# One level of Strassen's algorithm in the MLP down-projection of a two-layer hybrid DiT block

## The chip, the cores and the metric

The kernel runs on one core of a Trainium2 chip. The metric is the device time of one execution in microseconds (us). TensorE (PE) does the matrix products, VectorE (DVE), ScalarE (ACT) and GpSimd (POOL) the elementwise work, and SyncE (SP) issues the DMAs.

## The reference, cut to what matters

Two layers of a hybrid block run over 512 latent and 256 context tokens of width 1024, in fp32. Attention, convolution and a state space model come first; the change does not touch them. Behind them stands an MLP with a squared ReLU and 4096 hidden units. In layer 0 it is computed for latent and context rows, in layer 1 for latent rows alone.

```python
D_MODEL, SEQ, DEPTH, CTX_LEN = 1024, 512, 2, 256
D_FF = 4 * D_MODEL

def squared_relu_mlp(t, w1, w2):
    return jnp.square(jax.nn.relu(t @ w1)) @ w2
...
    for l in range(DEPTH):
        with_ctx_out = l < DEPTH - 1
...
        f_lat = squared_relu_mlp(modulate(rms_norm(h, g_pre_mlp), sh2, sc2), w_mlp_in[l], w_mlp_out[l])
        h = h + g2 * rms_norm(f_lat, g_post_mlp)
        if with_ctx_out:
...
            f_ctx = squared_relu_mlp(modulate(rms_norm(hc, g_pre_mlp), sh2c, sc2c), w_mlp_in[l], w_mlp_out[l])
```

## The kernel before

**Arithmetic.** An fp32 value is split into a high half, which is the value rounded to the matmul's fp32r type, and a low half, which is the rest. `mm3` (L638 to L641) forms a product by three matmuls: high times high, high times low, low times high.

**Weights.** They go through one ring of ten tiles of 128 x 1024, all named `w` (`wtile`, L610). `wload` (L614) loads raw tiles by SP's queue (L620), rounds each on ACT to a high tile (L623) and subtracts to a low tile (L624), on DVE and POOL in turn. So each weight tile passes three tiles of the ring. `blocks` (L630) gives the tiles of one call the shape that the products want.

**The MLP** (`phase_mlp`, from L1364) goes through the 4096 hidden units in eight groups of four blocks of 128. For a group, `get1` loads four blocks of `w_mlp_in`, and `mlp1` (L1383) computes a block of hidden values: 24 matmuls for the 512 latent columns and, in layer 0, 24 more for the 256 context columns. They end in PSUM tiles `ps_m`; ACT takes the ReLU (L1391), DVE squares (L1392), ACT and DVE split the result (L1394, L1395). `get2` loads four blocks of `w_mlp_out`. The down-projection then goes over the token tiles of 128 rows: 4 blocks x 3 matmuls in each of two halves of 512 output columns, into a PSUM tile `ps_q` of 1024 columns. DVE adds it to an accumulator in SBUF, `facc` (L1469; a tile named `g`). Group 0 copies in place of adding. Group 7 also has the output norm and the residual (L1463 and on).

**Beside it.** In layer 0, groups 1 to 3 carry steps that prepare layer 1's state space model (`E.npr`), and groups 4 to 7 the adaptive modulation of layer 1, eight raw tiles a group through the same ring with four small matmuls each (L755, `E.ada1`).

**The order.** Nothing is placed by hand: the tile scheduler sets each engine's order from the program text and its own estimates of time. PSUM has three tiles `ps_m`, one `ps_a` and two `ps_q` in this phase. A tile of a ring is free again when its last reader is done, and a load into it waits for that.

## Time and profile before

| | |
|---|---|
| time, median of 3 runs | 1655.72 us (1654.39 to 1658.1) |
| time of the profiled execution | 1657.21 us |
| its span in the trace | 1655.4 us |
| mean granted TensorE clock | 0.969 of full speed |
| PE busy | 1559.4 us, 94%, 8872 matmuls |
| DVE busy | 900.2 us, 54% |
| ACT busy | 552.5 us, 33% |
| POOL busy | 302.5 us, 18% |
| loads of w_mlp_in, w_mlp_out | 64 of 512 KB each |

The span is what the trace covers; the time of the same execution is 1.8 us longer. Busy shares are means over all stages of the kernel, and a matmul's busy time includes its overlap with the next, so the distance between starts tells its price. All rows below are of this one execution.

### The profile page before, as it was taken

To read this page: it belongs to the slowest core of one execution; us is meant where nothing else is said; L and a number is where in the kernel's file an instruction comes from. 1 tells how busy PE (TensorE), PEld (TensorE's weight loads), DVE (VectorE), ACT (ScalarE), POOL (GpSimd) and SP (SyncE) were. 2 spreads that over 40 slices of the span, in tenths; PEclk is the share of its full clock that TensorE was granted. 3 is DMA by queue.
4 is the path that set the end of the run, shared out by engine and by line. 5 is a ranking of instruction groups with operands and counts; after the bars stand their busy time and mean duration, and the time that the engine had idled before them with its cause. 6 is when DMAs were issued, how large, how long until landed. Compare 5 with 4: busy or idle time off the path is not lost.

```text
span 1655.4 us, 22621 instructions
## 1 busy us (share of the span) xinstructions
PE 1559.4 (94%) x8872; PEld 1258.4 (76%) x8872; DVE 900.2 (54%) x1986; ACT 552.5 (33%) x1037; POOL 302.5 (18%) x231
## 2 busy tenths in 40 slices
PE   5899999899999999999999988999898999999997
PEld 2677876667888888877788866687676888888885
DVE  8776538677965553232333376753775733333335
ACT  5321235655413213030321344212564433322222
POOL 0000221022211111110111135013102322212222
PEclk9999999999999999999999998979899999999999
DMA  9466311015232222263511245831203232222223
GB/s 347 144 217 212 112 52 52 1 52 186 97 112 87 94 70 77 98 225 112 203 51 51 91 187 177 303 110 54 100 1 113 92 102 92 90 98 102 102 89 127
DMA packets 72986, 193.80 MB, mean 117 GB/s; under 512 B 15152, under 2 KB 25648, under 8 KB 72496
## 3 DMA queue, kind: packets, MB, share of 16 engines
q1 hardware_dynamic: 72880, 192.37, 33.4%
q8 instruction: 69, 1.13, 0.3%
q14 instruction: 37, 0.30, 0.1%
HBM read 172.15 MB, written 20.19 MB: 116 GB/s over the span
## 4 chain that ended last, share of the span: by engine, by line
PE 77%; DVE 13%; ACT 4%; DMA 3%; issue 2%; POOL 1%; SPq 0%; DVEq 0%; ACTq 0%; POOLq 0%
PE ps_m L639 14%; PE ps_m L641 14%; PE ps_m L640 14%; PE ps_q L640 8%; PE ps_q L639 8%; PE ps_q L641 8%; PE ps_a L755 3%; ACT p L872 2%; PE ps_s L526 2%; PE ps_t L897 2%; DVE p L864 1%; DMA w<-in_w_ada 1%; DVE p L877 1%; PE ps_t L890 1%; DMA ssm_tr<-strips 1%
## 5 line engine op out<-in xcount | busy, mean ns | idle before, releaser
L624 POOL TENSOR_TENSOR w<-w 128x1024 fp32r<-128x1024 f32 x79 | 193.1, 2444 | 785.9 <-ACT w L623 345.0
L623 ACT CAST w<-w 128x1024 fp32r<-128x1024 f32 x172 | 179.0, 1050 | 454.0 <-PE ps_q L640 293.2
L640 PE MATMUL ps_q<-w,f 128*128 128x512 f32 x640 | 249.1, 391 | 1.9 <-DVE w L624 1.1
L639 PE MATMUL ps_q<-w,f 128*128 128x512 f32 x640 | 247.4, 392 | 2.9 <-DVE g L1463 2.6
L641 PE MATMUL ps_q<-w,f 128*128 128x512 f32 x640 | 247.2, 390 | 0.0
L624 DVE TENSOR_TENSOR w<-w 128x1024 fp32r<-128x1024 f32 x93 | 115.9, 1247 | 150.2 <-ACT w L623 136.7
L639 PE MATMUL ps_m<-g,w 128*128 128x256 f32 (+1 forms) x544 | 177.3, 331 | 2.4 <-DVE g L712 2.4
L640 PE MATMUL ps_m<-g,w 128*128 128x256 f32 (+1 forms) x544 | 178.9, 330 | 0.0
L641 PE MATMUL ps_m<-g,w 128*128 128x256 f32 (+1 forms) x544 | 177.1, 329 | 0.0
L640 PE MATMUL ps_m<-f,w 128*128 128x512 f32 (+1 forms) x464 | 170.4, 368 | 0.3 <-POOL f L715 0.3
L641 PE MATMUL ps_m<-f,w 128*128 128x512 f32 (+1 forms) x464 | 170.3, 368 | 0.0
L639 PE MATMUL ps_m<-f,w 128*128 128x512 f32 (+1 forms) x464 | 170.0, 371 | 0.0
L1469 DVE TENSOR_TENSOR g<-g,ps_q 128x1024 f32<-128x1024 f32 x60 | 73.3, 1221 | 177.1 <-PE ps_q L641 177.1
L639 PEld LDWEIGHTS ps_q<-w,f 128*128 128x128 f32 x640 | 119.9, 188 | 29.1 <-DVE g L1463 3.9
L640 PEld LDWEIGHTS ps_q<-w,f 128*128 128x128 f32 x640 | 120.5, 188 | 27.5 <-DVE w L624 2.0
L641 PEld LDWEIGHTS ps_q<-w,f 128*128 128x128 f32 x640 | 120.5, 188 | 24.9
L639 PE MATMUL ps_m<-w,f 128*128 128x512 f32 (+1 forms) x336 | 124.0, 371 | 8.9 <-DVE p L917 4.0
L641 PE MATMUL ps_m<-w,f 128*128 128x512 f32 (+1 forms) x336 | 123.4, 369 | 0.0
L640 PE MATMUL ps_m<-w,f 128*128 128x512 f32 (+1 forms) x336 | 121.8, 364 | 0.0
L1392 DVE SCALAR_TENSOR_TENSOR relu<-ps_m,relu 128x512 f32<-128x512 f32 (+1 forms) x104 | 58.5, 565 | 115.9 <-ACT relu L1391 115.6
L639 PEld LDWEIGHTS ps_m<-g,w 128*128 128x128 f32 x544 | 103.1, 192 | 16.0 <-DVE g L712 3.0
L640 PEld LDWEIGHTS ps_m<-g,w 128*128 128x128 f32 x544 | 104.2, 192 | 11.5 <-issue 1.6
(285 smaller groups left out, 2557.5 us busy)
## 6 DMA issues: line engine op xcount, KB each, us to landing
w<-in_w_ada SPq DMA_DIRECT2D x88, 512.0 KB
w<-in_w_mlp_in SPq DMA_DIRECT2D x64, 512.0 KB
w<-in_w_mlp_out SPq DMA_DIRECT2D x64, 512.0 KB
w<-in_w_out SPq DMA_DIRECT2D x16, 512.0 KB
w<-in_w_conv SPq DMA_DIRECT2D x12, 512.0 KB
h_d<-g SPq DMA_DIRECT2D x12, 512.0 KB
w<-in_w_q SPq DMA_DIRECT2D x8, 512.0 KB
f<-h_d SPq DMA_DIRECT2D x8, 512.0 KB
```

The source lines that it names most:

```text
L526: nc.tensor.matmul(out(g), U[d].o[rows, q, k].rearrange("p t i -> p (t i)"), sp[d][rows, q, k, lo:NCH], start=False, stop=d == 1 and q == ...
L623: nc.scalar.copy(hi, raw)
L624: (nc.gpsimd if turn % 2 and E.wpool else nc.vector).tensor_sub(lo, raw, hi.bitcast(F32))
L639: nc.tensor.matmul(out, lh, rh, start=first, stop=False)
L640: nc.tensor.matmul(out, lh, rl, start=False, stop=False)
L641: nc.tensor.matmul(out, ll, rh, start=False, stop=last)
L755: nc.tensor.matmul(pa[32 * b:32 * b + 32, k * 256:(k + 1) * 256], E.cT[:, kc], raw[k][:, b * 256:(b + 1) * 256], start=kc == 0 and k == 0, ...
L864: V.tensor_tensor_reduce(out=p[i][:, :nk * P], in0=pq[:, l0:768], in1=E.mask[:, moff:moff + nk].rearrange("p a b -> p (a b)"), scale=0.125 ...
L872: nc.scalar.activation(p[i][:, :nk * P], p[i][:, :nk * P], AF.Exp, bias=nm[:, i:i + 1], accum_out=sm[:, i:i + 1])
L897: nc.tensor.matmul(po[e * 64:(e + 1) * 64, :256], vv, pr[:, :, e], start=j == 0, stop=j == nk - 1)
L1392: V.scalar_tensor_tensor(out=s, in0=pt, scalar=0.0, in1=s, op0=OP.max, op1=OP.mult)
L1469: V.tensor_add(facc[t], facc[t], pq)
```

## The change

In groups 1 to 6 of both layers the latent rows' down-projection is done by one level of Strassen's algorithm in Winograd's form. The 512 token rows, the 512 hidden units of the group and the 1024 output columns are each halved. Seven products of quarters, or of sums and differences of quarters, take the place of eight. A product here is `times`: 2 token tiles x 2 hidden blocks x 3 matmuls of 512 columns. Three PSUM tiles collect them (X, Y, Z, from the two buffers `ps_q`), and partly accumulated tiles are added to the accumulators on DVE, 14 sums of 512 columns a group in place of 4 of 1024.

The sums of weight quarters are taken in place in the raw tiles (`w2_forms`), the sums of hidden quarters in the fp32 hidden tiles (`h_forms`). Each of the seven forms (eight in layer 0, which needs r12 for the context) is then split by `halves_split`, the weights' low halves on DVE and POOL in turn. In layer 1 three of the weight forms have tiles of their own (`wx`, six of 128 x 1024); in layer 0 all go through the ring of ten. Context rows keep the plain product (`plain`), and their up blocks now all come ahead of the latent ones. Groups 0 and 7 stay as they were.

```diff
@@ -641,6 +641,76 @@
     nc.tensor.matmul(out, ll, rh, start=False, stop=last)
+def halves_split(E, wt, src, turn):
+    hi, lo = (wt([P, 2, 512], F32R) for _ in range(2))
+    for i, x in enumerate(src):
+        E.nc.scalar.copy(hi[:, i], x)
+        (E.nc.gpsimd if (i + turn) % 2 else E.nc.vector).tensor_sub(lo[:, i], x, hi[:, i].bitcast(F32))
+    return hi, lo
+def w2_forms(E, views, ctx):
+    nc = E.nc
+    V = nc.vector
+    raw = []
+    for v in views:
+        raw.append(wtile(E, [P, 1024]))
+        nc.sync.dma_start(raw[-1], v)
+    q = {(j, n): [raw[2 * j + i][:, n * 512:(n + 1) * 512] for i in range(2)] for j in range(2) for n in range(2)}
+    def sub(o, x, y):
+        for i in range(2):
+            V.tensor_sub(q[o][i], q[x][i], q[y][i])
+    F = {}
+    wx = E.wx if E.nwx else lambda s, d: wtile(E, s, d)
+    wt = lambda s, d: wtile(E, s, d)
+    F["r11"] = halves_split(E, wt, q[0, 0], 0)
+    F["r21"] = halves_split(E, wt, q[1, 0], 1)
+    if ctx:
+        F["r12"] = halves_split(E, wt, q[0, 1], 0)
+    F["r22"] = halves_split(E, wx, q[1, 1], 1)
+    sub((0, 0), (0, 1), (0, 0))
+    sub((0, 1), (1, 1), (0, 1))
+    sub((1, 1), (1, 1), (0, 0))
+    F["t2"] = halves_split(E, wt, q[1, 1], 0)
+    F["t1"] = halves_split(E, wx, q[0, 0], 1)
+    sub((1, 0), (1, 0), (1, 1))
+    F["t3"] = halves_split(E, wt, q[0, 1], 0)
+    F["t4"] = halves_split(E, wx, q[1, 0], 1)
+    return F
+def h_forms(E, hf):
+    nc = E.nc
+    V = nc.vector
+    q = {(i, j): hf[j][:, :, i * 256:(i + 1) * 256] for i in range(2) for j in range(2)}
+    F = {}
+    def split(name, x):
+        f = E.f4([P, 2, 2, 256], F32R)
+        nc.scalar.copy(f[:, 0], x)
+        V.tensor_sub(f[:, 1], x, f[:, 0].bitcast(F32))
+        F[name] = f
+    split("l11", q[0, 0])
+    split("l12", q[0, 1])
+    split("l22", q[1, 1])
+    V.tensor_add(q[1, 1], q[1, 0], q[1, 1])
+    V.tensor_sub(q[1, 0], q[0, 0], q[1, 0])
+    V.tensor_sub(q[0, 0], q[1, 1], q[0, 0])
+    split("s2", q[0, 0])
+    split("s1", q[1, 1])
+    split("s3", q[1, 0])
+    V.tensor_sub(q[0, 1], q[0, 1], q[0, 0])
+    split("s4", q[0, 1])
+    return F
 def sq_sum(E, x, acc, dump=None):
     if dump is None:
         dump = E.sm.tile([P, 512], BF16, name="dump", tag="dump", bufs=2)[:, :x.shape[1]]
@@ -932,6 +1002,7 @@
     E.nada, E.ada1 = 2, {4: 4, 5: 4, 6: 4, 7: 4}
     E.steps = ((0, 2, 2, 5, 8), (1, 1, 1, 3, 4))
     E.npr = {1: 3, 2: 2, 3: 2}
+    E.fast = (range(1, 7), range(1, 7))
     with ExitStack() as ctx:
         E.cst = ctx.enter_context(tc.tile_pool(name="cst", bufs=1))
         E.sm = ctx.enter_context(tc.tile_pool(name="sm", bufs=1))
@@ -1380,6 +1451,80 @@
     ada = ada_steps()
     prep = ssm_spill(E) if l == 0 else iter(())
+    E.nwx = 0 if both else 6
+    E.wx = lambda shape, dt: E.g4p.tile(shape, dt, name="wx", tag="wx", bufs=E.nwx)
+    def strassen(g):
+        hf = [E.f4([P, 2, NL]) for _ in range(2)]
+        hx = [E.f4([P, 4, NCX], F32R) for _ in range(2)] if both else None
+        def up(c, w, sg):
+            n, A = (NL, aL) if sg == 0 else (NCX, aC)
+            pt = E.pt('m')[:, :n]
+            for kc in range(8):
+                mm3(nc, pt, w[0][:, kc], w[1][:, kc], A(0, kc), A(1, kc), kc == 0, kc == 7)
+            s = E.t2([P, 512])[:, :n]
+            nc.scalar.activation(s, pt, AF.Relu)
+            o = s if sg else hf[c // 2][:, c % 2]
+            V.scalar_tensor_tensor(out=o, in0=pt, scalar=0.0, in1=s, op0=OP.max, op1=OP.mult)
+            if sg:
+                nc.scalar.copy(hx[0][:, c], s)
+                V.tensor_sub(hx[1][:, c], s, hx[0][:, c].bitcast(F32))
+        w = []
+        for k in range(2):
+            w.extend(blocks(E, w1, g * 4 + k * 2, 2, 8))
+            for _ in range(E.ada1.get(g, 0)):
+                next(ada, None)
+        for _ in range(E.npr.get(g, 0)):
+            next(prep, None)
+        for sg in ((1, 0) if both else (0,)):
+            for c in range(4):
+                up(c, w[c], sg)
+        R = w2_forms(E, [w2[g * 4 + c] for c in range(4)], both)
+        L = h_forms(E, hf)
+        def plain(hf_):
+            cs = slice(hf_ * 512, (hf_ + 1) * 512)
+            for t in (4, 5):
+                js = slice((t % 4) * P, (t % 4 + 1) * P)
+                pt = E.pt('m')
+                for c in range(4):
+                    r = R[f"r{c // 2 + 1}{hf_ + 1}"]
+                    mm3(nc, pt, hx[0][:, c, js], hx[1][:, c, js], r[0][:, c % 2], r[1][:, c % 2], c == 0, c == 3)
+                V.tensor_add(facc[t][:, cs], facc[t][:, cs], pt)
+        X, Y, Z = (E.pt('q') for _ in range(3))
+        def times(bank, l, r, first, i, n):
+            cs = slice(n * 512, (n + 1) * 512)
+            f, (rh, rl) = L[l], R[r]
+            for th in range(2):
+                o = bank[:, th * 512:(th + 1) * 512]
+                js = slice(th * P, (th + 1) * P)
+                for c in range(2):
+                    kw = dict(skip_group_check=True)
+                    nc.tensor.matmul(o, f[:, 0, c, js], rh[:, c], start=first and c == 0, stop=False, **kw)
+                    nc.tensor.matmul(o, f[:, 0, c, js], rl[:, c], start=False, stop=False, **kw)
+                    nc.tensor.matmul(o, f[:, 1, c, js], rh[:, c], start=False, stop=c == 1, **kw)
+            for th in range(2):
+                a_ = facc[2 * i + th][:, cs]
+                V.tensor_add(a_, a_, bank[:, th * 512:(th + 1) * 512])
+        if both:
+            plain(0)
+        times(X, "l11", "r11", True, 0, 0)
+        times(Y, "l12", "r21", True, 0, 0)
+        if both:
+            plain(1)
+        times(X, "s2", "t2", False, 0, 1)
+        times(Z, "s1", "t1", True, 1, 1)
+        times(X, "s3", "t3", False, 1, 1)
+        times(Z, "s4", "r22", False, 0, 1)
+        times(X, "l22", "t4", False, 1, 0)
     def mlp1(h1, c, w, sg, part=None):
         n, A = (NL, aL) if sg == 0 else (NCX, aC)
         ts = part if part else slice(0, n)
@@ -1387,7 +1532,7 @@
         pt = E.pt('m')[:, :n]
         for kc in range(8):
             mm3(nc, pt, w[0][:, kc], w[1][:, kc], A(0, kc, ts), A(1, kc, ts), kc == 0, kc == 7)
-        s = E.g4p.tile([P, 512], F32, name="relu", tag="relu", bufs=2)[:, :n]
+        s = E.t2([P, 512])[:, :n]
         nc.scalar.activation(s, pt, AF.Relu)
         V.scalar_tensor_tensor(out=s, in0=pt, scalar=0.0, in1=s, op0=OP.max, op1=OP.mult)
         hi, lo = (h1[sg][q](c)[:, ts] for q in range(2))
@@ -1404,6 +1549,9 @@
         return h1
     for g in range(8):
+        if g in E.fast[l]:
+            strassen(g)
+            continue
         h1 = h1_tiles()
         ws = []
         w = []
```

The scheduler places the rest. In the names below `w` is a tile of the weights' ring, `f4` a tile of hidden values, `g4` an accumulator or an input column tile, `ps_m` and `ps_q` are PSUM tiles.

The first place is DVE in layer 1, from the last hidden block of a group into its down-projection. Before:

```order
L1392 SCALAR_TENSOR_TENSOR relu_13328<-ps_m_13303,relu_13328 128x512
L1395 TENSOR_TENSOR f4_13206<-relu_13328,f4_13204 128x512
L1392 SCALAR_TENSOR_TENSOR relu_13358<-ps_m_13333,relu_13358 128x512
L1395 TENSOR_TENSOR f4_13206<-relu_13358,f4_13204 128x512
L1469 TENSOR_TENSOR g4_11715<-g4_11715,ps_q_13375 128x1024
L1469 TENSOR_TENSOR g4_11742<-g4_11742,ps_q_13401 128x1024
L1469 TENSOR_TENSOR g4_11769<-g4_11769,ps_q_13427 128x1024
L624 TENSOR_TENSOR w_13488<-w_13483,w_13487 128x1024
```

Now, in the last such place (ps_m_13879 is the last hidden block, ps_q_13990 is X, ps_q_13991 is Y, f4_13968 is the form l12, w_14100 the low half of the next group's first w_mlp_in tile):

```order
L1470 SCALAR_TENSOR_TENSOR f4_13770<-ps_m_13879,t2_13904 128x512
L649 TENSOR_TENSOR w_13954<-w_13907,w_13953 128x512
L1514 TENSOR_TENSOR g4_12051<-g4_12051,ps_q_13990 128x512
L1514 TENSOR_TENSOR g4_12078<-g4_12078,ps_q_13990 128x512
L697 TENSOR_TENSOR f4_13968<-f4_13770,f4_13968 128x512
L697 TENSOR_TENSOR f4_13971<-f4_13770,f4_13971 128x512
L703 TENSOR_TENSOR f4_13770<-f4_13769,f4_13770 128x2x256
L624 TENSOR_TENSOR w_14100<-w_14095,w_14099 128x1024
L704 TENSOR_TENSOR f4_13769<-f4_13769 128x2x256
L1514 TENSOR_TENSOR g4_12051<-g4_12051,ps_q_13991 128x512
```

The low half of l12, which product 2 reads, now stands behind the two sums that wait for product 1, and the next group's low half behind both.

The second place is PE in the same group: the end of product 2 (Y) and the first matmuls of the next group's up-projection. Now:

```order
L1509 MATMUL ps_q_13991<-w_13921,f4_13968 128x512
L1510 MATMUL ps_q_13991<-w_13922,f4_13968 128x512
L1511 MATMUL ps_q_13991<-w_13921,f4_13968 128x512
L639 MATMUL ps_m_14119<-g4_11443,w_14099 128x512
L640 MATMUL ps_m_14119<-g4_11447,w_14099 128x512
L641 MATMUL ps_m_14119<-g4_11443,w_14100 128x512
```

The up-projection's first block stands right behind the second product; w_14099 is the high half of the tile whose raw load, w_14095, goes into the buffer that r11's form had, read by product 1 just ahead.

The third place is PE in layer 0, group 4, at the end of the second context block and the start of the third (L825 are the ada matmuls, L755 of the kernel before). Now:

```order
L825 MATMUL ps_a_6807<-w_6817,cT_74 32x256 x4
L639 MATMUL ps_m_6942<-g4_3744,w_6799 128x256
L640 MATMUL ps_m_6942<-g4_3746,w_6799 128x256
L641 MATMUL ps_m_6942<-g4_3744,w_6800 128x256
L825 MATMUL ps_a_6807<-w_6828,cT_74 32x256 x4
L825 MATMUL ps_a_6807<-w_6829,cT_74 32x256 x4
L825 MATMUL ps_a_6807<-w_6840,cT_74 32x256 x4
L825 MATMUL ps_a_6807<-w_6841,cT_74 32x256 x4
L639 MATMUL ps_m_6972<-g4_3743,w_6856 128x256
L640 MATMUL ps_m_6972<-g4_3745,w_6856 128x256
L641 MATMUL ps_m_6972<-g4_3743,w_6857 128x256
```

And before, between a context block and the latent block behind it:

```order
L755 MATMUL ps_a_6641<-w_6651,cT_74 32x256 x4
L641 MATMUL ps_m_6776<-g4_3744,w_6630 128x256
L639 MATMUL ps_m_6776<-g4_3744,w_6629 128x256
L640 MATMUL ps_m_6776<-g4_3746,w_6629 128x256
L641 MATMUL ps_m_6776<-g4_3744,w_6630 128x256
L639 MATMUL ps_m_6776<-g4_3744,w_6629 128x256
L640 MATMUL ps_m_6776<-g4_3746,w_6629 128x256
L641 MATMUL ps_m_6776<-g4_3744,w_6630 128x256
L641 MATMUL ps_m_6806<-f4_3747,w_6634 128x512
L755 MATMUL ps_a_6641<-w_6662,cT_74 32x256 x4
```

The ada matmuls, which were spread singly among the blocks, now stand together ahead of the third block, and blocks of 512 columns no longer lie between the blocks of 256.

## Rows read from the trace of the kernel before

**Rows 1.** Page: busy time of each engine, and the chain that ended last, by engine
```profile
PE 1559.4 (94%) x8872; PEld 1258.4 (76%) x8872; DVE 900.2 (54%) x1986; ACT 552.5 (33%) x1037; POOL 302.5 (18%) x231
PE 77%; DVE 13%; ACT 4%; DMA 3%; issue 2%; POOL 1%; SPq 0%; DVEq 0%; ACTq 0%; POOLq 0%
```
**Rows 2.** Windows, MLP of layers 0, 1: us, busy PE, PEld, DVE, ACT, POOL (count), clock, DMA, GB/s
```profile
490.00:970.00 480.00, 479.67 (x2615) 394.80 (x2614) 193.24 (x326) 115.58 (x183) 72.76 (x35) 1.00 0.32 110
1318.00:1622.00 304.00, 303.25 (x1337) 250.76 (x1338) 111.90 (x113) 89.95 (x112) 68.89 (x29) 1.00 0.30 104
```
**Rows 3.** Timeline of PE, layer 1: start us, us, line, op, tiles, shape [idle before <-releaser]
```profile
1399.81 0.39 PE L640 MATMUL ps_m<-g,w 128*128 128x512 f32 x1
...
1409.78 0.39 PE L640 MATMUL ps_q<-w,f 128*128 128x512 f32 x1
```
**Rows 4.** Timeline of DVE, layer 1: the first sum of a down-projection in two groups following
```profile
1367.60 1.22 DVE L1469 TENSOR_TENSOR g<-g,ps_q 128x1024 f32<-128x1024 f32 x1 [5.03 <-PE ps_q L641]
...
1411.12 1.22 DVE L1469 TENSOR_TENSOR g<-g,ps_q 128x1024 f32<-128x1024 f32 x1 [5.03 <-PE ps_q L641]
```
**Rows 5.** Groups by form, 1350 to 1590 us: form xcount | busy us, mean ns | idle before, releaser
```profile
L1469 DVE TENSOR_TENSOR g<-g,ps_q 128x1024 f32<-128x1024 f32 x22 | 26.8, 1220 | 61.6 <-PE ps_q L641 61.6
L624 DVE TENSOR_TENSOR w<-w 128x1024 fp32r<-128x1024 f32 x21 | 25.7, 1226 | 48.5 <-ACT w L623 47.2 <-DMA w<-in_w_mlp_out 1.3
L1392 DVE SCALAR_TENSOR_TENSOR relu<-ps_m,relu 128x512 f32<-128x512 f32 x23 | 15.9, 690 | 25.2 <-ACT relu L1391 25.2
L624 POOL TENSOR_TENSOR w<-w 128x1024 fp32r<-128x1024 f32 x22 | 53.2, 2419 | 181.1 <-ACT w L623 136.4 <-PE ps_m L641 44.7
L623 ACT CAST w<-w 128x1024 fp32r<-128x1024 f32 x42 | 43.7, 1052 | 132.9 <-PE ps_q L640 70.2 <-PE ps_m L640 20.4 <-PE ps_q L641 17.8
```
**Rows 6.** Groups of the whole span, same columns: a 512-wide sum, a 512-wide GpSimd operation
```profile
L1463 DVE TENSOR_TENSOR g<-g,ps_q 128x512 f32<-128x512 f32 x20 | 13.4, 684 | 12.2 <-PE ps_q L641 12.2
L1282 POOL TENSOR_TENSOR f<-f,f 128x512 f32<-128x512 f32 x10 | 13.5, 1357 | 143.2 <-ACT dump L647 143.2
```
**Rows 7.** Timeline of SP, then of ACT, layer 1: a pair of w_mlp_in loads and its casts
```profile
1424.03 0.80 SPq L620 DMA_DIRECT2D w<-in_w_mlp_in  x2
...
1427.42 1.05 ACT L623 CAST w<-w 128x1024 fp32r<-128x1024 f32 x1 [2.43 <-DMA w<-in_w_mlp_in]
1428.64 1.05 ACT L623 CAST w<-w 128x1024 fp32r<-128x1024 f32 x1 [0.17 <-DMA w<-in_w_mlp_in]
```
**Rows 8.** Timeline of ACT and DVE, layer 1: from a group's last up product to its low half
```profile
1403.18 0.60 ACT L1391 ACTIVATE relu<-ps_m 128x512 f32<-128x512 f32 x1 [1.71 <-PE ps_m L641]
...
1405.19 0.90 DVE L1395 TENSOR_TENSOR f<-relu,f 128x512 fp32r<-128x512 f32 x1 [0.69 <-ACT f L1394]
```
**Rows 9.** Timeline of DVE and POOL, layer 0: one form alone, and beside a subtraction on GpSimd
```profile
444.49 0.68 DVE L447 TENSOR_TENSOR ssm_m<-ssm_pw,ssm_c 128x512 f32<-128x512 f32 x1
449.37 2.48 POOL L624 TENSOR_TENSOR w<-w 128x1024 fp32r<-128x1024 f32 x1 [6.58 <-ACT w L623]
449.90 2.50 DVE L447 TENSOR_TENSOR ssm_m<-ssm_pw,ssm_c 128x512 f32<-128x512 f32 x1
```
**Rows 10.** Timeline of PE, start of layer 1's MLP: 256-column matmuls, at full clock
```profile
1312.80 0.28 PE L639 MATMUL ps_m<-g,w 128*128 128x256 f32 x1
...
1315.56 0.28 PE L641 MATMUL ps_m<-g,w 128*128 128x256 f32 x1
```
**Rows 11.** The chain that ended last, one piece of layer 0: start us, us, what
```profile
1066.81 1.42 PE ps_a L755 x20
```
**Rows 12.** Windows, layer 1, and timeline of PE in it: a wait, and matmuls after it
```profile
1280.00:1290.00 10.00, 8.27 (x43) 7.01 (x44) 9.89 (x21) 4.89 (x10) 4.54 (x4) 0.61 0.50 179
1280.05 1.11 PE L700 MATMUL ps_q<-ident,g 128*128 128x128 f32 x4 [4.61 <-ACT g L673]
1286.30 0.41 PE L639 MATMUL ps_m<-g,w 128*128 128x256 f32 x1
...
1287.37 0.41 PE L641 MATMUL ps_m<-g,w 128*128 128x256 f32 x1
```

## The prediction

> **What bounds the kernel now.** I read the busy shares and the chain that ended last first. TensorE is busy for 94% of the span and carries 77% of the chain; VectorE is at 54%, ScalarE at 33%, GpSimd at 18% [rows 1]. The change lies in the MLP phases, so I then read those stretches alone. In 480 us of layer 0's MLP TensorE is busy for all but 0.33 us, in 304 us of layer 1's for all but 0.75 us, at a granted clock of 1.00, which is the 2.4 GHz level [rows 2]. There is no stall to win there: the time falls only with matmuls taken out, and every wait on PE that the change brings is lost in full. The other engines have room by their sums: in layer 1's stretch DVE is busy for 111.9 of 304 us [rows 2]. What matters is which of their results PE will find late.
>
> The prices of a matmul come from the timelines. Between the two rows of [rows 3] lie 44 steps of 512 columns: 9.97 / 44 = 0.2266 us each. Between those of [rows 10] lie 23 steps of 256 columns: 2.76 / 23 = 0.12 us. A matmul of the ada steps costs 1.42 / 20 = 0.07 us [rows 11]. A layer 1 group takes 1411.12 - 1367.60 = 43.5 us [rows 4], which is 192 matmuls (96 up, 96 down) at 0.2266.
>
> **What is removed.** Seven products of 12 matmuls (2 token halves, 2 hidden blocks, 3 of a split product) stand for 96: 84 remain. That is 12 x 0.2266 = 2.72 us per group, in 12 groups 144 matmuls and 32.6 us, all on PE, all on the path. The Trainium skill (TensorE: Matmul & The Clock Gate, Part 1) states 215.7 ns from one warm 512-column matmul to the next; by that the removal would be 31.1 us. The row says 0.2266 and I stay with it.
>
> **What is added beside PE, layer 1.** Before, DVE is busy for 111.9 / 304 x 43.5 = 16 us of a group [rows 2]: 4 sums of 1.22, 4 squares of 0.69, 4 low halves of weights of 1.23 [rows 5] and 4 of hidden blocks. After, it has 44 instructions of 512 elements (14 sums into the accumulators, 4 squares, 7 low halves of weights, 8 quarter differences, 7 low halves and 4 sums for the hidden forms). The nearest row is the 512-wide sum of 0.684 in group 7 [rows 6]; so 44 x 0.68 plus 2 low halves of w_mlp_in of 1.23 give 32.4 us. GpSimd goes from 4 x 2.42 = 9.7 us [rows 5] to 2 x 2.42 plus 7 of 1.36 (the nearest row, [rows 6]) = 14.4 us. Both sums are under 43.5, so by sums alone they are hidden. They cost where something on DVE stands in a bad place.
>
> **Waits, layer 1.** The first w_mlp_in tile of the next group goes into the buffer of r11's form, so its load waits until product 1 is nearly through; PE needs its high half 14 matmuls later and its low half 16 later, 16 x 0.2266 = 3.6 us. Before, weights are loaded well ahead. The load takes 1427.42 - 1424.03 = 3.4 us from issue to cast, the cast 1.05 [rows 7], the subtraction 1.23 [rows 5], with 0.3 for the steps between: 6.0 us. PE waits 6.0 - 3.6 = 2.4 us in each group. The second wait falls in the same place and partly under the first. The low half of l12 stands on DVE behind the two sums of product 1, and those wait for all its 12 matmuls (2.7 us). So it is ready 2.7 + 2 x 0.68 + 0.68 = 4.8 us after product 1 begins, while product 2 wants it after 14 x 0.2266 = 3.2: a wait of 1.6 us where before the chain from the last product to the low half (1403.18 to 1406.09, 2.9 us [rows 8]) ran with nothing between. In the order the subtraction of the new tile comes behind these too. What this, and the later forms of w_mlp_out, add to the 2.4 I bound by 0 and 1.35 and take 0.7. So 2.4 to 3.75, taken 3.1: per group -2.72 + 3.1 = +0.38, and **+2.3 us** for six. The first changed group of layer 1 meets a ring that is still full of group 0's splits; between nothing and one late load that nothing covers (3.4 + 1.05, about 4) I take **+2**.
>
> **Waits, layer 0.** Here the context's plain products lie between: 24 + 12 + 12 + 24 matmuls, 72 x 0.2266 = 16.3 us, cover the forms. About 26 DVE instructions must be through by then, at 0.68 some 17.7, part of them before the stretch. I take 0.7 (0.2 to 1.9) at the second product and 0.5 (0 to 1.0) at t3's low half, which stands behind sums: 1.2 per group (0.2 to 2.9). Groups 1 to 3: 3 x (-2.72 + 1.2) = **-4.6 us**.
>
> In groups 4 to 6 the eight ada tiles pass through the same ring of ten. With the context's four blocks now in a row, the third block's w_mlp_in load waits for an ada matmul, and PE reaches the block after 11 matmuls of 256 columns and 20 of ada: 11 x 0.12 + 20 x 0.07 = 2.7 us. The chain is 3.4 to 4.6 for the load (first and second of a pair [rows 7]), then 1.05 and 1.23. Its low half is needed two matmuls later, so PE waits between 3.1 and 4.2; I take 3.5, nearer to the first of a pair. Before, blocks of 512 and 256 columns alternate there and give more cover. 3 x (-2.72 + 1.2 + 3.5) = **+5.9 us**.
>
> **Sum.** -4.6 + 5.9 + 2.3 + 2 = +5.6 us. The profiled execution took 1657.2 (its span 1655.4), so 1662.8; the median of the runs shown, 1655.7, lies 1.5 lower, so against that **1661**. All low ends: -7.6 + 1.7 - 1.9 + 0 = -7.8, which is 1648. All high ends: +0.5 + 13.1 + 6.2 + 4 = +23.8, which is 1679.5. In other words the 32.6 us come off PE's work and about 38 come back as waits.
>
> **Rival A, faster: loads land in time.** The two loads of [rows 7] were in the air together, and their casts began 1.22 us apart. If a lone load lands that much sooner, in 2.2 us, each of the nine late loads (6 in layer 1, 3 in layer 0) costs 1.2 less; with DVE never late besides, the low ends fall by 10.8 to -18.6, which is 1637. With half of it, 1642. It decides from the point where a group's waits fall under 2.72 us. For it: windows of the trace show the DMA engines at 0.30 [rows 2]. Against it: part of 3.4 us is fixed, and in layer 1 something waits in the same place whatever the load does. Time 1642, chance 0.25.
>
> **Rival B, slower: the clock falls.** After a wait of 4.61 us PE ran 256-column matmuls 1.07 / 5 = 0.214 us apart, the 1.2 GHz level, and the window of 10 us was granted 0.61 [rows 12]. That lasts to 1287.37 at least, 7.3 us from the end of the wait at 1280.05; half of it, 3.7 us, is lost each time. The waits forecast in groups 4 to 6 come near that length; 3 x 3.7 = 11 more gives 1672 (all twelve groups, 1705). Against it: each of my waits is split over several places and shorter than 4.61. Chance 0.12.
>
> **Rival C, slower: DVE becomes the bound.** One form of DVE took 0.68 alone and 2.50 beside a GpSimd subtraction of 2.48 that began 0.53 earlier [rows 9]: DVE stood still meanwhile. If this holds for every DVE instruction with both inputs in SBUF, 26 x 0.68 + 2 x 1.23 = 20.1 us of these and GpSimd's 14.4 can't overlap; with the 18 that read PSUM (12.2) the group takes 46.7 us, 3.2 over today's 43.5. Six groups make +19 in place of +2.3: 1678. The Trainium skill (SBUF — State Buffer, "SBUF: two separate sides") calls the shared port pair "an exclusive lock, not a bandwidth split"; the trace agrees (2.50 against 0.68). Against it: GpSimd waits for ScalarE or PE for much of its time [rows 5], so part of its work falls where DVE is idle. Chance 0.13.
>
> **How the numbers follow.** The forecast has 0.50. A measurement of this kernel tells about 0.2% from no change, 3.3 us: "same" is 1652.4 to 1659.0. The forecast's own range of 1648 to 1679.5 is centred above it: of its 0.50 I give 0.30 to slower, 0.17 to same and 0.03 to faster. A's 0.25 goes to faster, B's and C's 0.25 to slower. Faster 0.28, same 0.17, slower 0.55. The range reaches from A's lowest, 1637, to a little past C, 1684; what lies beyond is B in many groups and A with nothing late.
>
> **What would show it.** PE should have 144 matmuls less. Right: in layer 1, between the end of product 1 and the next group's up-projection, waits on PE of 2.4 to 3.75 us per group released by the weights' cast or subtraction or by L697, and a period of 43 to 44.5 us in the first sum of a group; in layer 0's groups 4 to 6 a wait of 3 us or more at the third context block, and none so long in groups 1 to 3. C would show as DVE busy without gaps and a period near 46.7; B as a granted clock under 1.00 in the MLP's windows. The forecast is wrong if the period is under 42, or the ada groups show no wait on the weights.

## The result, and the profile after

The changed kernel takes 1705.9 us (median of 4 runs, 1703.2 to 1707.1) against 1656.9 us for the kernel before (4 runs), a ratio of 1.0293 (95% interval 1.0269 to 1.0316): 49 us slower. The prediction had said 1661, from 1637 to 1684. The profiled execution took 1707.07 us, its span is 1705.1 us, 49.7 more than before's.

The page of the changed kernel, busy times and the chain by engine:

```profile
PE 1559.6 (91%) x8728; PEld 1249.1 (73%) x8728; DVE 1124.6 (66%) x2364; ACT 622.7 (37%) x1205; POOL 384.3 (23%) x297
PE 67%; DVE 20%; ACT 5%; DMA 4%; issue 2%; POOL 1%; SPq 0%; DVEq 0%; ACTq 0%; POOLq 0%
```

The 144 matmuls are gone (8872 to 8728 [rows 1]), yet PE is busy as long as before: matmuls ran slower, at a mean granted clock of 0.952 against 0.969. The windows of both MLPs (columns as in [rows 2]) say the same. Layer 0's groups 1 to 6, then layer 1's:

```profile
496.80:968.70 471.90, 450.39 (x2439) 365.93 (x2438) 292.97 (x547) 146.79 (x259) 116.62 (x73) 0.98 0.31 107
1363.40:1668.00 304.60, 290.23 (x1228) 234.55 (x1227) 226.59 (x289) 118.50 (x187) 100.47 (x57) 0.97 0.30 102
```

Before, PE was idle there for 0.33 and 0.75 us at a clock of 1.00 [rows 2]; now for 21.5 and 14.4 us, at 0.98 and 0.97. What PE waited for in layer 1's window (us in total, times, longest):

```profile
PE ps_q L1511 <- DVE f L697: 8.8, 7, 1.8
PE ps_q L1509 <- ACT f L696: 5.3, 6, 1.5
PE ps_m L641 <- DVE w L624: 0.2, 1, 0.2
```

and in layer 0's (the longest six):

```profile
PE ps_q L1510 <- DVE w L649: 7.1, 9, 1.9
PE ps_q L1510 <- POOL w L649: 4.4, 3, 2.9
PE ps_m L639 <- ACT w L623: 4.2, 3, 2.0
PE ps_a L347 <- DVE f L337: 1.4, 1, 1.4
PE ps_q L1509 <- DVE g L1514: 1.3, 3, 0.6
PE ps_m L641 <- DVE w L624: 1.3, 2, 0.8
```

One boundary in layer 1, on PE's timeline and then on DVE's, shows how a wait arises and what follows it:

```profile
1629.06 0.50 PE L1509 MATMUL ps_q<-w,f 128*128 128x512 f32 x1 [0.72 <-ACT f L696]
1629.40 0.40 PE L1510 MATMUL ps_q<-w,f 128*128 128x512 f32 x1
1630.99 0.80 PE L1511 MATMUL ps_q<-w,f 128*128 128x512 f32 x1 [1.20 <-DVE f L697]
1631.58 0.63 PE L1509 MATMUL ps_q<-w,f 128*128 128x512 f32 x1
1632.01 0.63 PE L1510 MATMUL ps_q<-w,f 128*128 128x512 f32 x1
...
1634.48 0.39 PE L1510 MATMUL ps_q<-w,f 128*128 128x512 f32 x1
1634.71 0.39 PE L1511 MATMUL ps_q<-w,f 128*128 128x512 f32 x1
```

```profile
1628.45 0.69 DVE L649 TENSOR_TENSOR w<-w 128x512 fp32r<-128x512 f32 x1 [0.59 <-POOL w L649]
1629.06 1.28 DVE L1514 TENSOR_TENSOR g<-g,ps_q 128x512 f32<-128x512 f32 x2
1630.25 1.28 DVE L697 TENSOR_TENSOR f<-f,f 128x512 fp32r<-128x512 f32 x2
```

Product 2 waits for l12's high half, then for its low half, which stands on DVE behind the two sums of product 1. After these two waits of 0.72 and 1.20 us, matmuls start 0.43 us apart until 1634.1 (the 1.2 GHz level), then 0.23 again (the 2.4 GHz level): 1.7 us lost beside the waits.

To place the rest I matched the DVE instructions that both traces have, and took the difference of their start times at four points of before: at 400 us (ahead of layer 0's MLP), 980 (its end), 1280 (ahead of layer 1's MLP) and the end. The same was done for the experiments' profiles:

| us over before in | to 400 | layer 0 MLP | layer 1 mixer | layer 1 MLP |
|---|---|---|---|---|
| changed kernel | 2.1 | 26.7 | 7.4 | 13.6 |
| e1 no Strassen | 10.3 | 9.5 | -1.0 | 2.4 |
| e2 layer 0 | 7.9 | 27.3 | 7.1 | 3.6 |
| e3 layer 1 | -0.3 | 9.8 | 2.9 | 10.8 |
| e4 own ReLU | 5.9 | 12.1 | 3.4 | 8.6 |
| e5 fill | 2.2 | 14.1 | 1.0 | 2.4 |
| e6 short chain | 1.6 | 17.6 | 4.5 | 39.5 |
| e7 forms on DVE | 1.5 | 14.0 | -6.2 | 9.4 |
| e8 alternate | 2.3 | 8.8 | 2.9 | 8.4 |
| e9 defer | 5.1 | 14.8 | 6.1 | 34.4 |
| e10 defer, DVE | 0.5 | 13.7 | -1.0 | 34.3 |
| e11 and alternate | -1.7 | 1.1 | 4.9 | 31.5 |
| e12 layer 1 only | 4.2 | -0.1 | -0.5 | 31.8 |
| e13 sums behind | 7.6 | 13.3 | 5.5 | 1.7 |
| e14 layer 1 only | 5.3 | 0.0 | -0.8 | 2.3 |
| e15 best of | 5.9 | -4.7 | 3.0 | 3.3 |
| e16 layer 1 filled | 2.0 | 0.0 | 7.0 | 2.2 |
| e17 best, filled | -0.1 | -4.1 | 3.0 | 1.4 |
| e18 layer 0 only | -0.9 | -4.5 | 3.1 | -0.3 |

No kernel changes the work of the first column, which still varies by 12 us, nor that of the mixer, which varies by 14. Nearly all of the latter arises in one stretch, 1050 to 1130 us of before. e14 and e16 are alike up to there, yet the stretch took 79.7 us at a granted clock of 0.87 in the one and 86.3 at 0.80 in the other. In before, then e14, then e16:

```profile
1050.00:1130.00 80.00, 79.27 (x614) 64.25 (x613) 52.00 (x94) 15.74 (x28) 10.38 (x14) 0.87 0.47 162
1055.20:1134.90 79.70, 79.37 (x614) 64.36 (x613) 52.17 (x94) 16.12 (x28) 10.32 (x14) 0.87 0.47 163
1052.00:1138.30 86.30, 85.34 (x614) 70.02 (x613) 52.03 (x94) 16.09 (x28) 10.41 (x14) 0.80 0.45 151
```

Whole times therefore tell little under 0.4%. The two MLP columns tell much more, for kernels that are alike in a layer agree there within 3 us (layer 0 in e4, e5 and e9: 12.1 to 14.8), and I read the experiments by them. They come from one profile of each kernel. Beside the experiments the kernel before itself ran from 1652 to 1671 us.

### The profile page after: what moved, and what is told of

Read it like the earlier page. It is cut to its first block, busy times and chain, and to the rows that moved or that the text cites. A ratio compares the mean times of both kernels' runs of the same rounds, so it can differ in the third digit from the quotient of the medians.

```text
span 1705.1 us, 23175 instructions
## 1 busy us (share of the span) xinstructions
PE 1559.6 (91%) x8728; PEld 1249.1 (73%) x8728; DVE 1124.6 (66%) x2364; ACT 622.7 (37%) x1205; POOL 384.3 (23%) x297
## 4 chain that ended last, share of the span: by engine, by line
PE 67%; DVE 20%; ACT 5%; DMA 4%; issue 2%; POOL 1%; SPq 0%; DVEq 0%; ACTq 0%; POOLq 0%
PE ps_m L639 14%; PE ps_m L640 13%; PE ps_m L641 13%; PE ps_q L1511 3%; PE ps_q L1510 3%; PE ps_q L1509 3%; PE ps_a L825 2%; ACT p L942 2%; PE ps_s L526 2%; PE ps_q L639 2%; DVE w L666 2%; DVE w L649 2%; PE ps_q L640 2%; PE ps_q L641 2%; PE ps_t L967 1%
## 5 line engine op out<-in xcount | busy, mean ns | idle before, releaser
L624 POOL TENSOR_TENSOR w<-w 128x1024 fp32r<-128x1024 f32 x55 | 137.9, 2508 | 376.0 <-ACT w L623 234.7
L623 ACT CAST w<-w 128x1024 fp32r<-128x1024 f32 x124 | 129.6, 1049 | 180.7 <-DMA w<-in_w_mlp_in 44.1
L649 POOL TENSOR_TENSOR w<-w 128x512 fp32r<-128x512 f32 x72 | 113.7, 1585 | 284.6 <-ACT w L648 277.9
L639 PE MATMUL ps_m<-w,f 128*128 128x512 f32 (+1 forms) x432 | 160.9, 376 | 8.9 <-DVE p L987 4.0
L641 PE MATMUL ps_m<-w,f 128*128 128x512 f32 (+1 forms) x432 | 161.1, 374 | 0.0
L640 PE MATMUL ps_m<-w,f 128*128 128x512 f32 (+1 forms) x432 | 160.0, 372 | 0.0
L1514 DVE TENSOR_TENSOR g<-g,ps_q 128x512 f32<-128x512 f32 x168 | 107.7, 680 | 58.0 <-PE ps_q L1511 57.9
L648 ACT CAST w<-w 128x512 fp32r<-128x512 f32 x144 | 82.4, 618 | 156.6 <-PE ps_m L640 75.0
L624 DVE TENSOR_TENSOR w<-w 128x1024 fp32r<-128x1024 f32 x69 | 84.2, 1222 | 67.3 <-ACT w L623 61.2
L639 PEld LDWEIGHTS ps_m<-g,w 128*128 128x128 f32 x544 | 107.9, 200 | 23.4 <-ACT w L623 4.8
L1510 PE MATMUL ps_q<-w,f 128*128 128x512 f32 x264 | 108.8, 412 | 11.5 <-DVE w L649 7.1
L641 PEld LDWEIGHTS ps_m<-g,w 128*128 128x128 f32 x544 | 108.0, 199 | 13.4 <-DVE w L624 2.7
L1511 PE MATMUL ps_q<-w,f 128*128 128x512 f32 x264 | 108.5, 411 | 8.8 <-DVE f L697 8.8
L640 PEld LDWEIGHTS ps_m<-g,w 128*128 128x128 f32 x544 | 108.4, 199 | 10.4 <-issue 1.2
L1509 PE MATMUL ps_q<-w,f 128*128 128x512 f32 x264 | 107.9, 410 | 7.5 <-ACT f L696 5.3
L649 DVE TENSOR_TENSOR w<-w 128x512 fp32r<-128x512 f32 x72 | 66.7, 926 | 60.5 <-ACT w L648 51.4
```

Source lines behind the costliest of these rows:

```text
L623: nc.scalar.copy(hi, raw)
L624: (nc.gpsimd if turn % 2 and E.wpool else nc.vector).tensor_sub(lo, raw, hi.bitcast(F32))
L639: nc.tensor.matmul(out, lh, rh, start=first, stop=False)
L640: nc.tensor.matmul(out, lh, rl, start=False, stop=False)
L641: nc.tensor.matmul(out, ll, rh, start=False, stop=last)
L648: E.nc.scalar.copy(hi[:, i], x)
```

## The experiments

**Which part, which layer (e1 to e4).** Beside Strassen the change moved the ReLU tile from two tiles of its own to the four tiles `t2`, which the transposes ahead of the MLP use too. It did so in `mlp1` as well, so groups 0 and 7 did not stay wholly as they were.

```diff
-    E.fast = (range(1, 7), range(1, 7))
+    E.fast = ((), ())
```

is e1; e2 and e3 empty one of the two ranges. e4 keeps both and undoes the move:

```diff
-        s = E.t2([P, 512])[:, :n]
+        s = E.g4p.tile([P, 512], F32, name="relu", tag="relu", bufs=2 if both else 1)[:, :n]
```

> No group by Strassen in either layer; what is left of the change is the ReLU tile, which is taken from the four tiles t2 that the transposes use too. Theory 1 (the shared tiles cost time outside the changed groups: in the changed kernel the traces drift apart by about 6.5 us up to the end of group 0 of layer 0, 7.4 us in layer 1's mixer and 3.4 us at the start of layer 1's MLP): 6 to 17 us over the kernel before. Rival (that drift comes from the scheduler's answer to the new products): within 3 us of the kernel before.

> Groups 1 to 6 of layer 0 alone by Strassen. If the account of the two traces holds (groups of layer 0 +22 us, drift around them 6.5 and 7.4 us): about 33 to 39 us over the kernel before, 1690 to 1696. Rival (the loss sits in layer 1, whose groups my sum put near zero): under 1675.

> Groups 1 to 6 of layer 1 alone. By the account of the two traces the layer 1 MLP costs 10.2 us from its first copy to the end, and 3.4 us ahead of it: 1668 to 1672 if the shared ReLU tiles cost nothing in layer 0; 1674 to 1684 if they do (theory 1).

> The changed kernel with the ReLU tile in tiles of its own again (two in layer 0, one in layer 1, where there is no room for two). Theory 1: 6 to 17 us less than the changed kernel, 1689 to 1700. Rival: 1703 to 1709, no different.

Measured against 1658.8 for the kernel before: e1 1674.4 (ratio 1.0079, 1.0053 to 1.0105), e2 1696.9 (1.0199), e3 1686.7 (1.0149), e4 1685.8 (1.0147, 1.0121 to 1.0173). In the table each layer's loss comes with that layer's own change: layer 0's column is 27.3 in e2 and 9.8 in e3, layer 1's 3.6 and 10.8 (e3 came out 3 us above the higher of its two ranges). So with no Strassen product at all the kernel loses 13 us, and with Strassen but ReLU tiles of its own the loss falls from 49 us to some 25 (27 by the medians, 24 by the ratio). e1's PE timeline shows the place, at the start of layer 0's MLP, where before had no wait over 1.7 us:

```profile
434.19 1.12 PE L770 MATMUL ps_q<-ident,g 128*128 128x128 f32 x4 [4.43 <-ACT g L743]
441.69 0.58 PE L639 MATMUL ps_m<-g,w 128*128 128x256 f32 x1 [1.58 <-DVE t L1537]
```

The ReLU's square (L1537) releases the PSUM tile that the next block wants, and the transposes (L770) no longer have hidden blocks to run beside. The changed kernel has the same two waits, 4.4 and 1.6 us; in e4 both are gone. From here on every kernel has its own ReLU tiles.

**The clock (e5).** Eight dead matmuls go between products 1 and 2 of each layer 1 group:

```diff
+        if not both:
+            pa = E.pt('a')
+            for _ in range(8):
+                nc.tensor.matmul(pa, L["l11"][:, 1, 1, P:], R["r11"][0][:, 0], start=True, stop=True)
         times(Y, "l12", "r21", True, 0, 0)
```

> e4_relu_own, with 8 dead matmuls of 512 columns put on PE between products 1 and 2 of each group of layer 1 (their result, in the spare PSUM tile, is read by nobody). They lie where PE waits 0.7 and 1.2 us for l12's halves and where four of six groups then ran some 8 matmuls at 1.2 GHz. Clock theory (the drop follows from PE having nothing to do there, and costs about 1.4 us a group beside the wait): the 48 dead matmuls (10.9 us) run inside the waits, no half clock is left, and the time is 5 to 10 us under e4, about 1.011 of before. Rival (the drop has another cause, and dead work is work): 0 to 10 us over e4.

Measured: 1676.2, ratio 1.0109 (1.0059 to 1.016); the intervals of e4 and e5 overlap, so the profiles decide. The same 240 us of layer 1 in e4 and in e5:

```profile
1400.00:1640.00 240.00, 229.88 (x981) 186.60 (x980) 187.36 (x245) 95.44 (x153) 81.92 (x47) 0.98 0.28 97
```

```profile
1400.00:1640.00 240.00, 238.06 (x1044) 195.05 (x1043) 186.76 (x246) 96.85 (x154) 80.94 (x47) 1.00 0.31 108
```

1044 matmuls against 981 in the same time. With 40 dead ones taken off, 1004 useful ones still beat 981. The waits there fell from 10.2 us to 1.9, in e4, then in e5:

```profile
PE ps_q L1511 <- DVE f L697: 6.0, 5, 1.2
PE ps_q L1509 <- ACT f L696: 4.2, 5, 1.3
```

```profile
PE ps_q L1511 <- DVE f L697: 1.9, 5, 0.4
```

The 40 dead matmuls (9.1 us) take the place of these waits, so they alone win nothing; what is won is the half clock, which went wholly. Layer 1's MLP costs 2.4 us in place of 8.6. The clock theory is shown here: with PE kept at work in these places, the drop doesn't come.

**Making the wait shorter (e6).** ScalarE squares and writes l12's high half straight from the ReLU, and GpSimd subtracts the last low half:

```diff
-            V.scalar_tensor_tensor(out=o, in0=pt, scalar=0.0, in1=s, op0=OP.max, op1=OP.mult)
...
+                if c > 1:
+                    nc.scalar.activation(l12[:, 0, c % 2], s[:, :256], AF.Square)
+                nc.scalar.activation(o, s, AF.Square)
+                if c > 1:
+                    (G if c == 3 else V).tensor_sub(l12[:, 1, c % 2], o[:, :256], l12[:, 0, c % 2].bitcast(F32))
```

> e4_relu_own, with the chain to l12 shortened in both layers: ScalarE squares in place of DVE, it writes l12's high half straight from the ReLU, and the low half of the last block is subtracted on GpSimd, so not behind the sums of product 1. Theory (layer 1's waits are this chain, and the clock loss follows them): waits on L696 and L697 gone, 1.9 + 0.3 + 1.1 us less in each of six groups: 12 to 20 us under e4, 1.003 to 1.007 of before. Rival (my forecast's late load of w_mlp_in, hidden so far behind this wait, takes its place at up to 2.4 us a group): 0 to 6 us under e4, with PE waiting for L623 or L624.

Measured: 1727.1, ratio 1.0408, far outside both. ScalarE's casts of the weight forms wait for DVE's low halves and stand ahead of l12's on its queue, so the high half came later than before (waits on it of 1.5 to 2.4 us), and the late w_mlp_in appeared as the rival had it. On PE's timeline, then DVE's, then GpSimd's:

```profile
1451.16 0.50 PE L641 MATMUL ps_m<-g,w 128*128 128x512 f32 x1 [2.29 <-DVE w L624]
```

```profile
1448.18 2.92 DVE L624 TENSOR_TENSOR w<-w 128x1024 fp32r<-128x1024 f32 x1
```

```profile
1447.67 2.35 POOL L624 TENSOR_TENSOR w<-w 128x1024 fp32r<-128x1024 f32 x1 [4.14 <-ACT w L623]
```

A subtraction that takes 1.23 alone [rows 5] takes 2.92 here, where GpSimd's had begun 0.5 us earlier, as in [rows 9].

**GpSimd's share, and the order of blocks (e7, e8).** e7 takes all low halves of the weight forms from GpSimd, e8 puts context and latent blocks of layer 0 in turn again:

```diff
-        (E.nc.gpsimd if (i + turn) % 2 else E.nc.vector).tensor_sub(lo[:, i], x, hi[:, i].bitcast(F32))
+        E.nc.vector.tensor_sub(lo[:, i], x, hi[:, i].bitcast(F32))
...
-        for sg in ((1, 0) if both else (0,)):
-            for c in range(4):
+        for c in range(4):
+            for sg in ((1, 0) if both else (0,)):
```

> e4_relu_own, with all low halves of the weight forms subtracted on DVE, none on GpSimd. If the shared port is what makes DVE late (forms of 0.68 stretched to 1.5 or more beside GpSimd): waits on L649 and L697 shrink and the time is 3 to 12 us under e4. If DVE's own amount of work is (90 instructions more, 0.6 us each, some 4.5 us a group): 5 to 40 us over e4.

> e4_relu_own, with context and latent blocks of layer 0's up-projection in turn again, as in the kernel before. If the context blocks in a row are why PE waits for w_mlp_in in groups 4 and 5 (1.8 + 0.8 us each, and some 1.5 us of half clock after it): 6 to 9 us under e4. Rival (the same load is late at another block, or the products now wait for the last context block): within 3 us of e4, or over it.

Measured: e7 1682.5 (1.0147, 1.0096 to 1.0198), e8 1680.0 (1.0123, 1.0078 to 1.0169). By its time e7 settles nothing, since its interval holds e4 and both of its cases; its profile says more. DVE, in e4, then in e7, by the page:

```profile
PE 1548.6 (92%) x8728; PEld 1239.2 (74%) x8728; DVE 1128.5 (67%) x2364; ACT 621.4 (37%) x1205; POOL 378.6 (22%) x297
PE 1542.8 (92%) x8728; PEld 1234.4 (74%) x8728; DVE 1126.2 (67%) x2454; ACT 620.4 (37%) x1205; POOL 245.1 (15%) x207
```

DVE took over 90 subtractions, 133 us of GpSimd's time, and was busy no longer: GpSimd's share had cost DVE as much as it spared it. PE's waits for the weight forms in layer 0's six groups fell, those on l12 did not (in five groups of layer 1, 6.0 us in e4 and 8.7 in e7). In layer 0, e4, then e7:

```profile
PE ps_q L1510 <- DVE w L649: 8.1, 12, 1.9
```

```profile
PE ps_q L1510 <- DVE w L649: 4.6, 15, 0.6
```

e8 lowers layer 0's column from 12.1 to 8.8, less than the 6 to 9 us expected. PE's waits from 690 to 940 us in e4, then in e8, show which ones went:

```profile
PE ps_q L1510 <- DVE w L649: 4.7, 8, 1.0
PE ps_m L639 <- ACT w L623: 3.6, 2, 1.8
PE ps_m L641 <- DVE w L624: 1.6, 2, 0.8
```

```profile
PE ps_q L1510 <- DVE w L649: 4.7, 8, 1.0
PE ps_m L639 <- ACT w L623: 0.9, 1, 0.9
```

The late w_mlp_in of groups 4 and 5 is due to the context blocks in a row, as the prediction had it; group 6 has no ada steps left and no such wait. e7 and e8 together (layer 0 of e11) bring layer 0 to 1.1, a larger fall than the two gave apart; why was not looked into.

**Useful work in the gap (e9 to e12).** The last product of a layer 1 group is held back until the next group's hidden blocks are done, and r11's form moves to a tile outside the ring.

```diff
-    F["r11"] = halves_split(E, wt, q[0, 0], 0)
+    F["r11"] = halves_split(E, E.f4 if E.nwx else wt, q[0, 0], 0)
...
+        while pend:
+            pend.pop()()
         R = w2_forms(E, [w2[g * 4 + c] for c in range(4)], both)
...
-        times(X, "l22", "t4", False, 1, 0)
+        last = lambda: times(X, "l22", "t4", False, 1, 0)
+        if (not both) and g + 1 in E.fast[l]:
+            pend.append(last)
+        else:
+            last()
```

> e4_relu_own, in layer 1 with the last product of a group (l22 times t4) held back to stand behind the next group's last up block, where it covers the chain to l12 with useful work, and with r11's form out of the weights' ring, so that the next w_mlp_in load no longer waits for product 1. Theory (layer 1 loses to the waits on l12 and the half clock after them): the waits on L696 and L697 go, the group falls from 44.2 to 41.0 to 41.8 us, 12 to 17 us under e4, 1.004 to 1.008 of before. Rival (DVE is late in any place, since beside GpSimd it stands still): other waits of 2 us or more a group take their place, 0 to 6 us under e4.

> e9_defer with no low half of a weight form on GpSimd. If the shared port is what is left: 3 to 10 us under e9. If DVE's own sum is near its bound: 0 to 8 us over e9.

> e10_defer_dve with context and latent blocks of layer 0 in turn again, as in e8. If the two are independent: 3 to 5 us under e10, as e8 stands to e4. Rival: no different from e10, since layer 0's loss is the forms and not the loads.

> e10_defer_dve with plain products in layer 0. If layer 0 is where the loss that is left lies (8 to 12 us there by e4's trace against before's) and layer 1 now keeps 1.7 to 2.5 us in each of six groups: 8 to 15 us under before, 0.991 to 0.995. Rival (layer 1 breaks even at best): 0.998 to 1.003.

Measured: 1714.6 (1.033), 1705.4 (1.0288), 1695.6 (1.023) and 1687.8 (1.018), the last far outside both of its ranges. Layer 1 costs 31 to 34 us in all four, with or without GpSimd (what e10 gains on e9 lies in the first and the mixer column); e11 stands under e10 by more than expected, since layer 0's column falls from 13.7 to 1.1. The rival of e9 was right, and worse than it said. In e9 product 2 waits for the PSUM tile of the product held back, 25.2 us in five times, since that product's sums stand on DVE behind the weight forms; in e12 PE waits for l12 and for the next w_mlp_in:

```profile
PE ps_q L1513 <- DVE g L1518: 25.2, 5, 5.0
```

```profile
PE ps_q L1515 <- DVE f L697: 11.7, 6, 3.7
PE ps_m L641 <- DVE w L624: 8.5, 3, 2.8
PE ps_m L639 <- ACT w L623: 4.2, 7, 1.5
```

**The place of two sums (e13, e14).** The sums of product 1 are queued on DVE behind l12's low half, on e7 (e13) and with layer 0 plain (e14).

```diff
+        F[name + "_lo"] = V.tensor_sub(f[:, 1], x, f[:, 0].bitcast(F32)).ins
...
-            for th in range(2):
...
+            with (E.tc.issue_after(L["l12_lo"]) if l == "l11" and not both else ExitStack()):
+                for th in range(2):
```

> e7_forms_on_dve with one thing changed in layer 1: on DVE the two sums of product 1 are queued behind the low half of l12, which product 2 waits for. If that place in the queue is the wait (1.6 to 1.9 us a group on L697 in e7, and half clock after it): the wait falls under 0.6 us, the half clock goes, 8 to 16 us under e7, 1.005 to 1.010 of before. Rival (DVE is late everywhere; the next product or the next w_mlp_in pays, as when the last product was held back): within 4 us of e7.

> e13 with plain products in layer 0. If layer 1's groups now fall to 42 to 43 us: 3 to 9 us under before, 0.994 to 0.998. Rival (the wait only moves): 1.000 to 1.008.

Measured: e13 1679.8 (1.0134, 1.0098 to 1.0169), by whole times no different from e7; but its layer 1 column is 1.7 against 9.4, and the first three columns, where the two kernels are alike, are 17 us longer in e13's execution. PE's waits on l12's low half (L697) over five groups in e7, then in e13:

```profile
PE ps_q L1511 <- DVE f L697: 8.7, 5, 1.9
```

```profile
PE ps_q L1511 <- DVE f L697: 2.2, 5, 0.5
```

e14 gives 1660.3 against 1657.9, ratio 1.0011 (0.9992 to 1.003): layer 1 breaks even, as its rival said. Both runs agree that the place in the queue was the wait on l12's low half; the high half's stays at about 1 us a group. With it, the waits on l12's halves in e14's layer 1 still come to some 10 us, and two of its six groups run at half clock after them, which eats most of the 16.3 us of matmuls taken out.

**The best that was found (e15 to e18).** e15 joins e13 and e8 and leaves group 1 of layer 0 plain; e16 and e17 are e14 and e15 with 5 dead matmuls in e5's place; e18 is e15 with layer 1 plain (`E.fast = (range(2, 7), ())`).

> The parts that helped, together: ReLU tiles of their own, no weight form's low half on GpSimd, context and latent blocks of layer 0 in turn, the sums of product 1 behind l12 in layer 1, and group 1 of layer 0 plain (in e11 it alone lost 4 us, the other five gained 0.8 to 1.1 each). Layer 0 then gains 4 to 5 us, layer 1 what e14 shows: 0.990 to 0.996 of before. Rival (what the profile of e11 shows for layer 0 is given back in the mixer behind it): no gain from layer 0, time as e14.

> e14 with 5 dead matmuls between products 1 and 2 of each group of layer 1. In e14 PE waited there about 1.1 and 0.4 us, and in two of five groups half clock followed (1.8 us each). Clock theory: the 5 (1.13 us) run in the wait, the half clock goes, and a group takes (180 + 5) x 0.2266 + 0.5 = 42.4 us in place of 43.9: about 8 us under e14, 0.995 to 0.998 of before. Rival (in e14 the clock is not what is lost): 0 to 3 us over e14.

> e15 with the same 5 dead matmuls in layer 1. Layer 0's groups 2 to 6 gained 2.4 us in e15's profile, given back at the change of layers. With the fill: 6 to 9 us under e15, 0.994 to 0.998 of before. Rival: as e15, 1.000 to 1.003.

> e15 with plain products in layer 1: groups 2 to 6 of layer 0 alone. By e15's profile -2.4 us in the groups and +3.6 at the change of layers, so 0.999 to 1.002. Rival (the wait of 6.45 us at the change of layers is that one execution's): 0.996 to 0.999.

Measured: e15 1660.1 (1.0014, 0.9993 to 1.0036), e16 1661.1 (1.0012), e17 1659.8 (0.9998, 0.9979 to 1.0018), e18 1658.0 against 1659.1 (0.9986, 0.9969 to 1.0004). e15 to e17 fell short of what was expected, and the rivals came true. e16's says it: once the order is mended, dead matmuls cost what they save. In layer 0 five groups gain 4.1 to 4.7 us in three profiles (e15, e17, e18), and the mixer behind it takes back 3.0 in all three. It does so in the stretch shown above with the table; in e18:

```profile
1044.20:1128.70 84.50, 81.48 (x616) 66.66 (x611) 51.31 (x93) 15.02 (x27) 11.29 (x14) 0.82 0.45 154
```

```profile
PE ps_s L520 <- ACT ssm_tm L569: 3.0, 1, 3.0
```

PE waits 3.0 us there in all three (0.7 in before), and the granted clock is 0.82. Whether this follows from the changed layer 0 is open, for e16, whose layer 0 is plain, was slower there still. The wait of 6.45 us that the expectation of e18 names is not the cause, since the kernel before has it too, at the same transposes:

```profile
PE ps_m L700 <- DVE t L710: 8.0, 4, 6.5
```

No version clearly beats the kernel before; e18 comes nearest to it.

## Why the prediction was wrong, step by step

- **The removal** held: 144 matmuls less, 12 x 0.2266 a group. The 215.7 ns that the Trainium skill states (TensorE: Matmul & The Clock Gate, Part 1) are not what this kernel's matmuls take: the rows after show 0.23 us again.
- **The ReLU tile** is the step that was missing. The sum has no term for it and gives no reason, though the diff moves it. It costs 13 us alone (e1) and some 20 in the changed kernel (1705.9 less e4's 1685.8, and 19.6 by the two MLP columns).
- **The waits** came out near in sum, but by misses that cancel, which is luck. Layer 0: forecast 3 x 1.2 + 3 x (1.2 + 3.5) = 17.7 us, measured 21.5. Of it the third context block in the ada groups, forecast at 3 x 3.5 = 10.5, took 5.2 in two groups (the third has no ada steps left), and all else 16.3 where 7.2 were forecast, most of it at the weight forms' low halves. Layer 1: forecast 6 x 3.1 + 2 = 20.6, measured 14.4. Its main term, "PE waits 6.0 - 3.6 = 2.4 us in each group" for w_mlp_in, was wrong: 0.2 us in all. The wait on l12, put with the later forms at 0.7 a group, took 14.1, and 5.3 of that was for l12's high half, which the text does not name. It comes ahead of the wait for w_mlp_in, which appears at up to 2.8 us when the order changes (e6, e12). The place of l12's low half, behind the sums of product 1, was right, and e13 shows it.
- **The clock** was put at nothing in the sum. It stood as rival B, from the one row of a 4.61 us wait [rows 12], and the text held against it that "each of my waits is split over several places and shorter than 4.61". Waits of 0.72 and 1.20 us were enough, and rival B's own sign, a clock under 1.00 in the MLP's windows, is there. Summed over all starts that come late by more than half a matmul with no wait between, 13.3 us are lost in layer 0's window (4.9 before, beside the ada steps) and 8.7 in layer 1's (none before): some 17 us more. Rival B's figure for all twelve groups, 1705, is the measured time by coincidence, for it has 44 us of half clock in it. Each wait also costs about 0.17 us to start again.
- **The sum in the trace:** -32.6 for the matmuls, +35.9 of waits in the groups, +17 of half clock and +6 of restarts make some 26 us. The two MLP columns hold 40.3, so some 14 more lie in the MLPs but not in the changed groups' products, and e1, with 9.5 and 2.4 in these columns, shows where: at the start of either MLP, above all of layer 0's, with the ReLU tile. The other 9.5 lie ahead of 400 us and in the mixer (86.4 us at a clock of 0.80 in the stretch shown with the table), which differ as much between kernels that are alike there; that they come from the change is not shown.
- **Rival C** (DVE the bound) is half right. That DVE stands still beside GpSimd is shown (e6, e7). But DVE was busy for 226.6 of 304.6 us in layer 1, 74%, so its sum of work isn't the bound, and without GpSimd's share the time stayed (e7). Its forms come in bursts, and in a burst whatever is behind is late, as e9 to e12 show.

## What to carry to other kernels

When PE has no gap left, taking matmuls out can pay only if the engines that feed it are ahead at each boundary: look for what stands in front of the awaited instruction on its queue, not at the engine's busy share. Price every wait on PE with the slow matmuls that may follow. Price the small print of a change too: a tile moved into a shared pool cost as much here as the whole algorithm could have won in five groups. And work handed to a second engine helps only if the first does not stand still beside it.

## What the runs showed of the hardware

- PE fell to the 1.2 GHz level after two waits of 0.72 and 1.20 us within 2 us, but not each time: in e4 four of six groups with such waits were followed by 8 to 10 late matmuls, most of them 0.43 us apart (1.5 to 1.7 us lost), two were not.
- Dead matmuls in those places kept the clock at 1.00 and made layer 1's MLP 6.2 us shorter, not longer, where waits of 10.2 us were there to fill (e5 against e4); where less was to fill they won nothing (e16 against e14).
- GpSimd and DVE: subtractions with both inputs in SBUF took 2.92 and 3.28 us in place of 1.23 when one of GpSimd had begun before them (e6, e12). Taking 90 subtractions from GpSimd to DVE left DVE's busy time as it was, 1126.2 us against 1128.5 (e7 against e4).
- The same stretch of layer 1's mixer, with the same 614 matmuls, took 79.7 us at a granted clock of 0.87 and 86.3 at 0.80 in two executions (e14, e16).
